# Pinning the adaLN products of a hybrid decoder layer's mixer to slots in program order

## The chip, the cores and the metric

The kernel runs on one core of one Trainium2 chip. The metric is the device time of one execution in microseconds (us), as the median of several runs. Besides, one execution was recorded by the hardware profiler; its span runs from the first to the last instruction of the program.

## The reference, cut to what matters

One decoder layer for 256 tokens of width 1024, in float32. Three blocks follow each other, and each is fed by a normalised and modulated copy of the stream and gated back into it:

```python
mod = (c @ w_ada + b_ada).reshape(B, 9, D_MODEL)
sh1, sc1, g1, sh2, sc2, g2, sh3, sc3, g3 = [mod[:, None, i] for i in range(9)]
h = modulate(rmsnorm(x, ffn1_norm), sh1, sc1)
x = x + 0.5 * (1 + g1) * swiglu(h, ...)
h = modulate(rmsnorm(x, mix_norm), sh2, sc2)
x = x + (1 + g2) * hybrid_mixer(h, ...)
h = modulate(rmsnorm(x, ffn2_norm), sh3, sc3)
x = x + 0.5 * (1 + g3) * swiglu(h, ...)
return rmsnorm(x, final_norm)
```

The mixer projects h to q, k, v of an attention with 8 heads (one causal block of 256 tokens here), to x_m of an mLSTM with 4 heads (a causal convolution of 4 taps, a decay matrix, scores times decay, a normalisation) and to a gate z. The attention's output and the mLSTM's, the latter times silu(z), are concatenated and multiplied by w_out.

## The kernel before, in words

**Layout.** Channels lie on the 128 partitions and the 256 tokens on the free axis. The stream x is 8 tiles of 128x256, and the modulated copy h is kept as a high part `hh` and a low part `hl` of 8 tiles each, with two more columns for the shift.

**Products in three passes.** Every weight product (`mm3`) is three matmuls on TensorE: high weight by high input, low weight by high input, high weight by low input. Weights come in chunks of 128x2048 (`raw`, 4 buffers). `split_piece` (line 201) turns half a chunk into a high part `whi` on ScalarE (one copy) and a low part `wlo` on VectorE (one subtraction), with 5 buffers of 128x1024 for each. `weights()` (line 221) issues the loads up to three chunks ahead and the splits up to one chunk ahead of the chunk that it hands out.

**The adaLN products.** `mod` has 72 columns of 128. Each is one job: `ada(col)` (line 247) loads 128x1024 of w_ada (512 KB) into one of three `ada` buffers and forms the dot product with c in one VectorE instruction, whose full-size output `junk` is thrown away and whose sum goes to one column of `mod`. After 8 columns a few small instructions make the scale `gs`, the shift `sh` or the gate `gt`. The jobs stand in a list (line 571), and `side(...)` (line 564) takes one off it for each of its arguments; so the calls of `side` in the program say where a job is issued. In the mixer these calls stand at lines 933 to 1026; the first two calls belong to the product of x_m (line 579). The jobs left at that time are the gate of block 2, the scale `gs[2]` and the shift `sh[2]` of block 3.

**What sets the order.** A scheduler with its own timing model orders the instructions of each engine while the program is built (`schedule_with_timeline_sim`, line 42); what it decided is fixed then, and on the chip each engine takes its list in order. An instruction that was handed to `keep_in_program_order` is not moved against the others that were handed to it. All loads are (so SyncE's list is the program's order); of the compute engines' instructions those that were issued while the wrapper `Ordered` (line 45) was on for the engine. In the mixer it is off but for a stretch around `a_out` and `m_factors`. Each buffer has a few slots, so an instruction may also wait for a slot: a load of `ada` waits for the product that read the same slot three jobs before.

**The mixer's steps** (line 601 on). `tiles` runs one chunk of w_in as two products of 8 x 3 matmuls into a PSUM bank `psb`; `shifted` finishes such a product with a copy of the shift column (`col`, ScalarE), a product with the reciprocal root `rr` (`ht`, VectorE) and a copy with bias (ScalarE), and frees the bank. The rest is small: `gates` and `decays` make `rows` and the decay tiles `wE` from a chain on 4 partitions; `decays` spreads `rows` over two PSUM banks (TensorE, `psm<-rows,ohr`), subtracts into `wE` (VectorE, 8 instructions) and applies exp (ScalarE). `m_scores` multiplies keys by queries into a bank of the same pair (`psm<-qk,xc`) and the result into `wE`. `scores`, `turn`, `weigh` are the attention. The last chunk of w_in gives z; after it come `m_factors` (chain `dd`, `vv`, `rs` on 4 partitions, then `rows` again), `z_silu` in two halves, and `hilo` of the attention's output tiles `oa` into `hh`/`hl` 1 to 3, which hold h until the last product of z has read it. Then w_out runs in 8 steps of 24 matmuls: step 0 reads `mix0h`/`mix0l`, steps 1 to 3 read the attention's tiles in `hh`/`hl`, steps 4 to 7 the mLSTM's (`m_out`). Then `pre_shift(2)` writes the shift `sh[2]` into the extra columns of `hh`/`hl`, and `residual` adds the product to x and makes h of block 3.

Of the kernel before, what the change touches and what calls it, by code (L numbers as in the profile page):

```python
# [14 lines left out]
ALU = mybir.AluOpType  # L15
# [46 lines left out]
def layer(ctx: ExitStack, tc: tile.TileContext, i, out: bass.AP):  # L62
    nc = tc.nc
    act, dve, pool, pe = (Ordered(tc, e) for e in (nc.scalar, nc.vector, nc.gpsimd, nc.tensor))
# [14 lines left out]
    def nm(s):  # L79
        cnt[0] += 1  # L80
        return f"{s}_{cnt[0]}"
# [3 lines left out]
    def bank(tag):  # L85
        return psp.tile([P, 512], F32, tag=tag, name=nm("ps" + tag), bufs=BANKS[tag])
# [7 lines left out]
    def const(shape, dt, name):  # L94
        return cst.tile(shape, dt, tag=name, name=name)

    def dma(out, in_):
        return tc.keep_in_program_order(sp.dma_start(out, in_))  # L98
# [26 lines left out]
    c_bc = const([P, D], F32, "c_bc")  # L125
# [95 lines left out]
    def weights(ahead=3):  # L221

        n = used[0]
        used[0] += 1
        load_to(n + ahead)
        split_to(n + 1)
        return parts[n]
# [6 lines left out]
    def mm3(ps, w, b0, xh, xl, start, stop):  # L234
        hi, lo = part(w, b0, P)
        pe.matmul(ps, hi, xh, start=start, stop=False, skip_group_check=True)
        pe.matmul(ps, lo, xh, start=False, stop=False, skip_group_check=True)
        pe.matmul(ps, hi, xl, start=False, stop=stop, skip_group_check=True)


    mod = const([P, 72], F32, "mod")
# [2 lines left out]
    gt = [const([P, ND], F32, f"gt{k}") for k in range(3)]  # L244
    NCOL = [C_N1, C_N2, C_N3]

    def ada(col, on_pool=False):

        t = wp.tile([P, D], F32, tag="ada", name=nm("ada"), bufs=3)
        dma(t, i["ada"][col])  # L250
        junk = wp.tile([P, D], BF16, tag="junk", name=nm("junk"), bufs=1)
        dve.scalar_tensor_tensor(junk, t, 1.0, c_bc, ALU.mult, ALU.mult,
                                 accum_out=mod[:, col:col + 1])

    def ada_gate_fin(k):
        s0 = 24 * k + 16
# [40 lines left out]
    def rstd_of(parts, ones=None, tag="m", pre=True, mid=None):  # L297

        ps = bank(tag)[:, 0:T]
        for n, s in enumerate(parts):  # L300
            pe.matmul(ps, ones_m if ones is None else ones, s, start=(n == 0), stop=(n == len(parts) - 1))
        r = t256("rr", bufs=2)
        l = t256("rl", bufs=1)
        if pre:
            tables("natural_log_exp_and_others")
        act.activation(l, ps, AF.Ln, bias=eps_t)
        act.activation(r, l, AF.Exp, scale=-0.5)
        if mid:
            mid()
        newton(r, ps, [P, T], "x")  # L310
        return r
# [90 lines left out]
    def ffn(k, nxt):  # L402
        nfa = 3
        with tc.tile_pool(name=f"g{k}", bufs=1) as gp:
            g2 = gp.tile([P, NF, 2, T], F32R, name=f"g2{k}")
            gh, gl = g2[:, :, 0], g2[:, :, 1]
            if k == 0:
                half = gp.tile([P, 8, 2 * T], F32, name="half")

                def adas(d):  # L410
                    ada(d, d > 0)
                    ada(8 + d)
# [151 lines left out]
    def side(*on):  # L564

        for o in on:
            if jobs:
                jobs.pop(0)(o)
# [5 lines left out]


    px = [bank("a") for _ in range(4)]
    for c in range(2):
        w = weights()
        side(1, 0)
        for d4 in range(4):  # L580
            d = c * 4 + d4
            for h in range(NH):
                mm3(px[h][:, 0:W], w, d4 * 512 + h * P, hh[:, d], hl[:, d], start=(d == 0), stop=(d == 7))
            if d == 0:
                r = rstd_of([acc, nxt_sq[0]], pre=False)
    with tc.tile_pool(name="mix", bufs=1) as mp:
        mixer(tc, nc, i, mp, locals())


    with tc.tile_pool(name="fin", bufs=1) as fp:  # L590
# [10 lines left out]
def mixer(tc, nc, i, mp, L):  # L601
    act, dve, pool, pe, sp = L["act"], L["dve"], L["pool"], L["pe"], L["sp"]
# [6 lines left out]
    side, jobs = L["side"], L["jobs"]  # L609
# [4 lines left out]
    def tiles(*done):  # L614

        w = weights()
        for g in range(2):
            pb = bank("b")
            for d in range(8):
                mm3(pb[:, 0:W], w, (g * 8 + d) * P, hh[:, d], hl[:, d], start=(d == 0), stop=(d == 7))  # L620
            done[g](pb)
            yield

    def shifted(dst):

        def done(pb):
            col = tmp.tile([P, 1], F32, tag="col", name=nm("col"), bufs=3)
            act.activation(col, pb[:, T:T + 1], AF.Copy)
            t = t256("ht", bufs=3)
            dve.tensor_tensor(t, r, pb[:, 0:T], ALU.mult)  # L630
            act.activation(dst, t, AF.Identity, bias=col)
        return done
# [16 lines left out]
    def fold():  # L649

        pg = bank("a")
        for h in range(NH):
            pe.matmul(pg[:, h * 40:(h + 1) * 40], wT[:, h], wif[:, h * 3], start=(h == 0), stop=False,
                      skip_group_check=True)
            pe.matmul(pg[:, h * 40:(h + 1) * 40], wT[:, 4 + h], wif[:, h * 3 + 1], start=False, stop=True,
                      skip_group_check=True)
            pe.matmul(pg[:, 160 + h * 40:160 + (h + 1) * 40], wT[:, 8 + h], wif[:, h * 3 + 2], start=False,
                      stop=True, skip_group_check=True)
        act.activation(wfold[:, 0:320], pg[:, 0:320], AF.Copy)
        pqk = bank("a")  # L660
        for h in range(NH):
            pe.matmul(pqk[:, h * P:(h + 1) * P], wT[:, h], wT[:, 4 + h], start=(h == 0), stop=(h == NH - 1),
                      skip_group_check=True)
        act.activation(wfold[:, 320:832], pqk, AF.Copy, scale=float(P) ** -0.5)

        vmean = mt([P, NH], "vmean")
        dve.tensor_reduce(vmean, wv0, AX.X, ALU.add)
        dve.tensor_scalar(vmean, vmean, 1.0 / P, None, ALU.mult)
        for h in range(NH):
            dve.tensor_scalar(wv[:, h], wv0[:, h], vmean[:, h:h + 1], None, ALU.subtract)  # L670
# [134 lines left out]
    def m_factors():  # L805


        prow, em = st["prow"], st["em"]
        act.on = dve.on = True
        dd = mt([NH, T], "dd", tag="R2")  # L810
        act.activation(dd, prow[0:4, 0:T], AF.Square, scale=EPS ** 0.5)
        dve.tensor_tensor(dd, dd, em, ALU.max)
        vv = mt([NH, T], "vv", tag="R3")
        dve.scalar_tensor_tensor(vv, prow[0:4, T:2 * T], 1.0 / P, dd, ALU.mult, ALU.add)
        rs = mt([NH, T], "rs", tag="R1")
        act.activation(rs, vv, AF.Ln)
        act.activation(rs, rs, AF.Exp, scale=-0.5)
        newton(rs, vv, [NH, T], "r", 0.0)
        spread(rs)
# [4 lines left out]
    def mix(k):  # L824
        return mix0 if k == 0 else (hh[:, k, 0:T], hl[:, k, 0:T])
# [3 lines left out]
    def z_silu(h2):  # L829
        z2 = zs[:, 2 * h2:2 * h2 + 2]  # L830
        tc.keep_in_program_order(act.activation(z2, z2, AF.Silu))
# [23 lines left out]
    def queries(j):  # L855
        qa, ka = st["qk", j] = mt([P, T], "qa", bufs=2), mt([P, T], "ka", bufs=2)
        return tiles(shifted(qa), shifted(ka))
# [31 lines left out]
    def values(c):  # L889
        v = [t256("gm"), t256("gm")]  # L890
        yield from tiles(shifted(v[0]), shifted(v[1]))
        pt = bank("a")
        for s in range(2):
            for g in range(2):
                pe.transpose(pt[:, (s * 2 + g) * P:(s * 2 + g + 1) * P], v[g][:, s * P:(s + 1) * P], ident)
        act.activation(va[:, :, c * T:(c + 1) * T], pt.rearrange("p (s c) -> p s c", s=2), AF.Copy)
        yield
# [39 lines left out]
    conv(1)  # L937
    next(g)
    fold()
    side(1, 0)  # L940
    g = queries(1)
    conv(2)
    next(g)
    conv(3)
    next(g)
    g0 = values(0)
    side(0, 1)
    next(g0)
    gates()
    next(g0)  # L950
    scores(0)
    m_queries()
    g = queries(2)
    side(0, 1)
    next(g)
    next(g0)
    m_values()
# [2 lines left out]
    scores(1)  # L960
    turn(0)
    g = queries(3)
    side(0, 1)
    next(g)
    weigh(0)
    m_scores(0)
# [3 lines left out]
    scores(2)  # L970
    m_scores(2)
    g0 = values(1)
    side(0, 1)
    next(g0)
    weigh(1)
    scores(3)
# [3 lines left out]
    m_scores(3)  # L980
    m_sums(1)
    g = tiles(shifted(zs[:, 0]), shifted(zs[:, 1]))
    side(1, 0, 0)
    next(g)
    next(g0)
    turn(3)
# [10 lines left out]
    m_vars(1)  # L997
    m_vars(2)
    g = tiles(shifted(zs[:, 2]), shifted(zs[:, 3]))
    side(1)  # L1000
    next(g)
    m_vars(3)
    m_factors()
    z_silu(0)
    next(g)
    for j in range(1, 4):
        hilo(*mix(j), oa[:, j, 0:T])
    z_silu(1)
    for h in range(NH):
        m_out_pre(h)  # L1010
# [1 line left out]
    po = [bank(t) for t in ("m", "m", "a", "a")]  # L1012
    for c in range(4):
        w = weights()
        side(0)
        pe.on = c < 2
        for k2 in range(2):
            k = c * 2 + k2
            for d in range(8):
                mm3(po[d // 2][:, (d % 2) * T:(d % 2 + 1) * T], w, (k2 * 8 + d) * P, *mix(k),  # L1020
                    start=(c == 0 and k2 == 0 and d % 2 == 0), stop=(c == 3 and k2 == 1))
                if (k, d) == (2, 7):
                    m_spread()
                    for h in range(NH):
                        m_out(h)
    side(*[0] * len(jobs))
    L["pre_shift"](2)
    for d in range(8):
        nxt_sq[0] = residual(d, po[d // 2][:, (d % 2) * T:(d % 2 + 1) * T], L["gt"][1], 2)

# [85 lines left out]
```

## Time and profile before

| | |
|---|---|
| median of 3 runs | 543.53 us (543.39 to 544.7) |
| the profiled execution's own time | 542.25 us |
| its span | 540.5 us |
| TensorE busy (matmul) | 516.9 us, 96% of the span |
| VectorE busy | 424.1 us, 78% |
| ScalarE busy | 282.6 us, 52% |
| moved by DMA | 125.73 MB, mean 233 GB/s |

The page's columns: PE is TensorE's matmul, PEld its weight load, DVE VectorE, ACT ScalarE, POOL GpSimd, SP SyncE. Times are from the span's start. Nearly every compute instruction has line 55 (the wrapper), so instructions are told apart by their tiles. In the timeline a row's second number is the time of the instructions that it merges, and "x8" counts the profiler's records: an fp32 matmul leaves two or more. The end of a matmul is modelled, so its start to the next one's start is the safer reading. The first block lasts to about 205 us, the mixer to about 340, the second feed-forward block to the end.

### The profile page before, as it was taken

To read this page: it belongs to the slowest core of one execution; us is meant where nothing else is said; L and a number is where in the kernel's file an instruction comes from. 1 tells how busy PE (TensorE), PEld (TensorE's weight loads), DVE (VectorE), ACT (ScalarE), POOL (GpSimd) and SP (SyncE) were. 2 spreads that over 40 slices of the span, in tenths; PEclk is the share of its full clock that TensorE was granted. 3 is DMA by queue.
4 is the path that set the end of the run, shared out by engine and by line. 5 is a ranking of instruction groups with operands and counts; after the bars stand their busy time and mean duration, and the time that the engine had idled before them with its cause. 6 is when DMAs were issued, how large, how long until landed. Compare 5 with 4: busy or idle time off the path is not lost.

```text
span 540.5 us, 9607 instructions
## 1 busy us (share of the span) xinstructions
PE 516.9 (96%) x3826; PEld 484.0 (90%) x3826; DVE 424.1 (78%) x717; ACT 282.6 (52%) x484; POOL 46.2 (9%) x60
## 2 busy tenths in 40 slices
PE   8999999999999999999969969999999999999992
PEld 7899999999988889978856869999999999988892
DVE  7899978988799988997894666979987777655433
ACT  4364456665554454648655544965554554544410
POOL 5000000000010210200010000400000000012320
PEclk9999999999999999999999979999999999999997
DMA  8999986587788985776771114387855455455002
GB/s 314 352 368 396 372 333 235 212 303 276 278 345 320 346 340 180 266 297 235 308 275 42 50 69 136 101 349 292 312 202 206 178 169 211 167 181 209 1 1 78
DMA packets 24095, 125.73 MB, mean 233 GB/s; under 512 B 2673, under 2 KB 3185, under 8 KB 14578
## 3 DMA queue, kind: packets, MB, share of 16 engines
q1 hardware_dynamic: 23762, 124.72, 61.6%
q8 instruction: 30, 0.49, 0.4%
q10 hardware_dynamic: 288, 0.39, 0.2%
q14 instruction: 15, 0.12, 0.1%
HBM read 124.05 MB, written 1.05 MB: 231 GB/s over the span
## 4 chain that ended last, share of the span: by engine, by line
PE 89%; DVE 4%; DMA 2%; ACT 2%; issue 1%; SPq 0%; DVEq 0%; ACTq 0%
PE psa L55 45%; PE psb L55 25%; PE psm L55 20%; DMA ada<-in_ada 2%; DVE junk L55 1%; ACT whi L55 1%; DVE wE L55 1%; DVE wlo L55 0%; DVE ht L55 0%; DVE u_out L55 0%; SPq L98 0%; ACT hh L55 0%; ACT L55 0%; ACT zs L55 0%; DVE nw L55 0%
## 5 line engine op out<-in xcount | busy, mean ns | idle before, releaser
L55 ACT ACTIVATE whi<-raw 128x1024 fp32r<-128x1024 f32 (+1 forms) x160 | 166.8, 1047 | 133.1 <-PE psa L55 83.4
L55 DVE TENSOR_TENSOR wlo<-raw,whi 128x1024 fp32r<-128x1024 f32 (+1 forms) x160 | 193.8, 1215 | 50.3 <-ACT whi L55 48.7
L55 PE MATMUL psa<-hh,wlo 128*128 128x256 f32 (+1 forms) x452 | 127.2, 282 | 0.0
L55 PE MATMUL psa<-hh,whi 128*128 128x256 f32 (+1 forms) x452 | 127.0, 283 | 0.0
L55 PE MATMUL psa<-hl,whi 128*128 128x256 f32 (+1 forms) x452 | 126.1, 281 | 0.0
L55 DVE SCALAR_TENSOR_TENSOR junk<-ada,c_bc 128x1024 bf16<-128x1024 f32 x72 | 89.4, 1242 | 8.3 <-DMA ada<-in_ada 7.7
L55 PEld LDWEIGHTS psa<-hh,wlo 128*128 128x128 f32 x452 | 85.9, 190 | 0.1
L55 PEld LDWEIGHTS psa<-hh,whi 128*128 128x128 f32 x452 | 85.7, 190 | 0.0
L55 PEld LDWEIGHTS psa<-hl,whi 128*128 128x128 f32 x452 | 85.5, 190 | 0.0
L55 PE MATMUL psb<-hh,whi 128*128 128x258 f32 (+1 forms) x284 | 81.6, 288 | 0.6 <-ACT whi L55 0.6
L55 PE MATMUL psb<-hh,wlo 128*128 128x258 f32 (+1 forms) x284 | 80.2, 283 | 0.6 <-DVE wlo L55 0.6
L55 PE MATMUL psb<-hl,whi 128*128 128x258 f32 (+1 forms) x284 | 79.8, 283 | 0.0
L55 PE MATMUL psa<-g,whi 128*128 128x512 f32 (+1 forms) x198 | 59.8, 369 | 0.0
L55 PEld LDWEIGHTS psb<-hh,whi 128*128 128x128 f32 x284 | 53.7, 189 | 2.7 <-issue 1.0
L55 PEld LDWEIGHTS psb<-hh,wlo 128*128 128x128 f32 x284 | 53.8, 189 | 0.9 <-DVE wlo L55 0.8
L55 PEld LDWEIGHTS psb<-hl,whi 128*128 128x128 f32 x284 | 53.5, 189 | 0.2 <-issue 0.2
L55 PE MATMUL psm<-hh,whi 128*128 128x256 f32 (+1 forms) x168 | 48.1, 287 | 4.8 <-ACT hh L55 4.8
L55 PE MATMUL psm<-hh,wlo 128*128 128x256 f32 (+1 forms) x168 | 47.8, 285 | 0.0
L55 PE MATMUL psm<-hl,whi 128*128 128x256 f32 (+1 forms) x168 | 47.5, 285 | 0.0
L55 PE MATMUL psa<-g,wlo 128*128 128x256 f32 x176 | 45.9, 281 | 0.0
L55 PEld LDWEIGHTS psa<-g,whi 128*128 128x128 f32 x198 | 35.2, 188 | 6.2
L55 PEld LDWEIGHTS psm<-hh,whi 128*128 128x128 f32 x168 | 32.5, 194 | 5.1 <-ACT hh L55 5.0
(238 smaller groups left out, 759.5 us busy)
## 6 DMA issues: line engine op xcount, KB each, us to landing
ada<-in_ada SPq DMA_DIRECT2D x72, 512.0 KB, 5.8
raw<-in_dn SPq DMA_DIRECT2D x22, 1024.0 KB, 4.8
raw<-in_guB SPq DMA_DIRECT2D x19, 1024.0 KB, 4.8
raw<-in_gu SPq DMA_DIRECT2D x18, 1024.0 KB, 6.4
raw<-in_gu SPq DMA_DIRECT2D x8, 512.0 KB, 7.3
raw<-in_wqk SPq DMA_DIRECT2D x4, 1024.0 KB, 5.4
raw<-in_wout SPq DMA_DIRECT2D x4, 1024.0 KB, 6.8
raw<-in_guA SPq DMA_DIRECT2D x4, 768.0 KB, 4.0
```

What stands on the lines that cost most here:

```text
L55: r = f(*a, **k)
```

## The change

The change has five edits. (1) While `pinned[0]` is true, that is from the product of x_m to the mixer's end, each adaLN product is handed to `keep_in_program_order`. (2) The calls of `side` are dealt out anew: fewer jobs at the start of the mixer and among the attention's products, five ahead of the first chunk of z, four ahead of the second, three in w_out's loop. (3) `z_silu(0)` moves behind the `hilo` of the attention's tiles. (4) w_out's loop takes no job in its first two turns and two, then three (as far as there are any) in its last. (5) `pre_shift(2)` runs with the wrapper on, for ScalarE and VectorE.

```diff
+    pinned = [False]
...
-        dve.scalar_tensor_tensor(junk, t, 1.0, c_bc, ALU.mult, ALU.mult,
-                                 accum_out=mod[:, col:col + 1])
+        p = dve.scalar_tensor_tensor(junk, t, 1.0, c_bc, ALU.mult, ALU.mult, accum_out=mod[:, col:col + 1])
+        if pinned[0]:
+            tc.keep_in_program_order(p)
...
     px = [bank("a") for _ in range(4)]
+    pinned[0] = True
     for c in range(2):
         w = weights()
-        side(1, 0)
+        side(*[0] * (2 - c))
...
         mixer(tc, nc, i, mp, locals())
+
+    pinned[0] = False
...
     fold()
-    side(1, 0)
+    side(0)
...
     g0 = values(0)
-    side(0, 1)
+    side(0)
...
     g = tiles(shifted(zs[:, 0]), shifted(zs[:, 1]))
-    side(1, 0, 0)
+    side(0, 0, 0, 0, 0)
...
     g = tiles(shifted(zs[:, 2]), shifted(zs[:, 3]))
-    side(1)
+    side(0, 0, 0, 0)
     next(g)
     m_vars(3)
     m_factors()
-    z_silu(0)
     next(g)
     for j in range(1, 4):
         hilo(*mix(j), oa[:, j, 0:T])
+    z_silu(0)
     z_silu(1)
...
     for c in range(4):
         w = weights()
-        side(0)
+        side(*[0] * c if c > 1 else ())
...
     side(*[0] * len(jobs))
+    act.on = dve.on = True
     L["pre_shift"](2)
+    act.on = dve.on = False
```

The scheduler then orders everything else anew. Three places follow; the numbers behind the names count buffers and differ between the two programs for the same tile.

VectorE, from the last attention maxima ahead of the decay tiles to the first scores times decay. Before:

```order
L55 COPY nac_2549<-psm_3010 128x8
L55 SCALAR_TENSOR_TENSOR junk_3406,mod<-ada_3404,c_bc 128x1024
L55 TENSOR_TENSOR em_2872<-nM_2868,F_2864 4x256
L55 TENSOR_TENSOR rows_2545<-nM_2868,rows_2545 4x256
L55 TENSOR_REDUCE mx_3315<-psa_3305 128x1 x2
L55 TENSOR_SCALAR mx_3224<-mx_3224 128x4
L55 TENSOR_TENSOR ht_3445<-rr_2420,psb_3418 128x256
L55 TENSOR_REDUCE mx_3315<-psa_3306 128x1 x2
L55 SCALAR_TENSOR_TENSOR junk_3551,mod<-ada_3549,c_bc 128x1024
L55 TENSOR_TENSOR wlo_3560<-raw_3256,whi_3559 128x1024
L55 TENSOR_SCALAR em_2872<-em_2872 4x256
L55 SCALAR_TENSOR_TENSOR wE_394_2550<-psm_3014,nac_2549,maskt 128x256
```

With the change:

```order
L55 TENSOR_TENSOR rows_2541<-nM_2856,rows_2541 4x256
L55 TENSOR_SCALAR pr_3062<-pr_3062,ri_3064 128x256
L55 SCALAR_TENSOR_TENSOR junk_3090,mod<-ada_3088,c_bc 128x1024
L55 TENSOR_SCALAR em_2860<-em_2860 4x256
L55 TENSOR_TENSOR ht_3129<-rr_2420,psb_3102 128x256
L55 COPY nac_2545<-psm_2994 128x8
L55 TENSOR_TENSOR wlo_3236<-raw_2936,whi_3235 128x1024
L55 TENSOR_TENSOR ht_3176<-rr_2420,psb_3149 128x256
L55 SCALAR_TENSOR_TENSOR wE_392_2546<-psm_2998,nac_2545,maskt 128x256
```

The first decay tile (wE) moved forward against the products of w_in: it stood behind the `ht` of the first product of z (psb_3418), and now stands behind that of the second half of q and k 3 (psb_3149), three products earlier. Ahead of it VectorE's list holds 11 adaLN products (`junk`) fewer than before; behind it, up to the end of w_out, 13 where there were 2. TensorE's list has the spreading of `rows` directly ahead of the first scores before (`psm<-rows,ohr`, then `psm<-qk,xc`), and with the change 14 matmuls of a product of w_in and 11 small ones of the attention between the two.

ScalarE, behind the chain of `m_factors`. Before:

```order
L55 ACTIVATE whi_3726<-raw_3553 128x1024
L55 ACTIVATE rows_2545<-rs_3599 4x256
L55 ACT_TABLE_LOAD
L55 ACTIVATE zs_2557<-zs_2557 128x512
L55 ACTIVATE col_3634<-psb_3609 128x1
L55 ACTIVATE zs_2557<-ht_3636,col_3634 128x256
L55 ACTIVATE hh<-oa_2559 128x256 x3
```

With the change:

```order
L55 ACTIVATE whi_3718<-raw_3549 128x1024
L55 ACTIVATE rows_2541<-rs_3595 4x256
L55 ACTIVATE col_3629<-psb_3604 128x1
L55 ACTIVATE zs_2553<-ht_3631,col_3629 128x256
L55 ACTIVATE hh<-oa_2555 128x256 x3
L55 ACT_TABLE_LOAD
L55 ACTIVATE zs_2553<-zs_2553 128x512 x2
```

The table load and the first silu stood between `rows` and the last `col`; they now stand behind the three `hh` tiles. On VectorE the same stretch, from the `ht` of the second product of z on, holds with the change:

```order
L55 TENSOR_TENSOR ht_3520<-rr_2420,psb_3493 128x256
L55 SCALAR_TENSOR_TENSOR junk_3535,mod<-ada_3533,c_bc 128x1024
L55 TENSOR_TENSOR ht_3586<-rr_2420,psb_3559 128x256
L55 SCALAR_TENSOR_TENSOR junk_3539,mod<-ada_3537,c_bc 128x1024
L55 TENSOR_TENSOR wlo_3661<-raw_3392,whi_3660 128x1024
L55 TENSOR_TENSOR dd_3590<-dd_3590,em_2860 4x256
L55 SCALAR_TENSOR_TENSOR junk_3543,mod<-ada_3541,c_bc 128x1024
L55 SCALAR_TENSOR_TENSOR vv_3593<-psa_3306,dd_3590 4x256
L55 SCALAR_TENSOR_TENSOR junk_3547,mod<-ada_3545,c_bc 128x1024
```

The four `junk` rows are new there; before, that list ran without them, and behind `vv` it held the two small instructions of `pre_shift`, which are now behind the last `ht` of w_out. On SyncE's list the loads of these four products (ada_3533 to ada_3545) now stand ahead of the load of w_out's third chunk (raw_3549), and five others ahead of its second.

## Rows read from the trace of the kernel before

**Rows 1.** Waits of TensorE from 205 to 360 us: total, times, longest.
```profile
PE psm L55 <- DVE wE L55: 4.9, 2, 4.2
PE psm L55 <- ACT hh L55: 4.8, 1, 4.8
```

**Rows 2.** Stretches: length, PE, PEld, DVE, ACT, POOL busy, PEclk, DMA share, GB/s.
```profile
232.00:260.00 28.00, 28.00 (x201) 23.33 (x198) 24.47 (x52) 20.12 (x47) 0.18 (x1) 1.00 0.74 278
276.00:287.00 11.00, 6.06 (x26) 4.32 (x25) 10.94 (x31) 7.19 (x24) 0.00 (x0) 0.84 0.55 210
287.00:311.00 24.00, 24.00 (x170) 19.35 (x169) 11.03 (x27) 13.16 (x32) 0.72 (x1) 1.00 0.09 32
304.20:314.20 10.00, 7.59 (x60) 6.81 (x58) 6.28 (x12) 6.61 (x13) 0.00 (x0) 1.00 0.22 79
316.50:322.50 6.00, 5.95 (x27) 5.95 (x28) 4.26 (x11) 1.52 (x4) 0.00 (x0) 0.50 0.17 65
322.50:330.00 7.50, 7.50 (x62) 7.24 (x62) 5.47 (x12) 3.58 (x6) 0.00 (x0) 0.99 0.07 11
```

**Rows 3.** Timeline of TensorE around the first wait: start, us, instruction, idle before.
```profile
277.12 0.73 PE L55 MATMUL psm<-rows,ohr 36*128 36x256 f32 x4
282.05 2.95 PE L55 MATMUL psm<-qk,xc 128*128 128x256 f32 x8 [4.20 <-DVE wE L55]
285.74 0.92 PE L55 MATMUL psm<-qk,xc 128*128 128x256 f32 x4 [0.74 <-DVE wE L55]
```

**Rows 4.** Timeline of VectorE in the same place.
```profile
278.15 1.22 DVE L55 SCALAR_TENSOR_TENSOR junk<-ada,c_bc 128x1024 bf16<-128x1024 f32 x1
279.29 1.23 DVE L55 TENSOR_TENSOR wlo<-raw,whi 128x1024 fp32r<-128x1024 f32 x1
280.62 2.67 DVE L55 SCALAR_TENSOR_TENSOR wE<-psm,nac,maskt 128x256 f32<-128x256 f32 x8
```

**Rows 5.** Timeline of TensorE around the second wait.
```profile
311.51 0.28 PE L55 MATMUL psa<-mix0l,whi 128*128 128x256 f32 x1
316.55 0.58 PE L55 MATMUL psm<-hh,whi 128*128 128x256 f32 x1 [4.75 <-ACT hh L55]
```

**Rows 6.** Timeline of ScalarE in the second wait.
```profile
311.83 1.06 ACT L55 ACTIVATE whi<-raw 128x1024 fp32r<-128x1024 f32 x1 [0.98 <-PE psa L55]
313.21 1.28 ACT L55 ACT_TABLE_LOAD   x1
314.50 0.63 ACT L55 ACTIVATE zs<-zs 128x512 f32<-128x512 f32 x1
315.04 0.15 ACT L55 ACTIVATE col<-psb 128x1 f32<-128x1 f32 x1
```

**Rows 7.** Timeline of VectorE ahead of and in the second wait, parts.
```profile
305.56 0.42 DVE L55 TENSOR_TENSOR ht<-rr,psb 128x256 f32<-128x256 f32 x1 [1.37 <-ACT col L55]
...
312.92 1.23 DVE L55 TENSOR_TENSOR wlo<-raw,whi 128x1024 fp32r<-128x1024 f32 x1 [0.35 <-ACT whi L55]
314.18 0.41 DVE L55 TENSOR_TENSOR rows<-rs,rows 4x256 fp32r<-4x256 f32 x1
315.23 0.42 DVE L55 TENSOR_TENSOR ht<-rr,psb 128x256 f32<-128x256 f32 x1 [0.64 <-ACT col L55]
```

**Rows 8.** DMA issues from 205 to 365 us: count, KB each, median us to landing.
```profile
ada<-in_ada SPq DMA_DIRECT2D x22, 512.0 KB, 3.7
raw<-in_wout SPq DMA_DIRECT2D x4, 1024.0 KB, 6.8
```

**Rows 9.** Timeline of VectorE and TensorE in w_out's later steps and behind them.
```profile
328.85 0.76 DVE L55 TENSOR_TENSOR hl<-ht,hh 128x256 fp32r<-128x256 f32 x2
...
340.31 0.48 DVE L55 SCALAR_TENSOR_TENSOR hl<-x,gs,hh 128x256 fp32r<-128x256 f32 x1
...
329.63 0.28 PE L55 MATMUL psm<-hl,whi 128*128 128x256 f32 x1
...
341.02 0.40 PE L55 MATMUL psb<-hl,whi 128*128 128x258 f32 x2
```

More of the change, by code (lines that the diff above doesn't have):

```diff
@@ L953, in mixer @@
     g = queries(2)
-    side(0, 1)
+    side(0)
     next(g)
@@ L962, in mixer @@
     g = queries(3)
-    side(0, 1)
+    side(0)
     next(g)
@@ L972, in mixer @@
     g0 = values(1)
-    side(0, 1)
+    side(0)
     next(g0)
```

## The prediction

> **What bounds the kernel now.** I read the waits of TensorE first, because the page has it busy for 96% of the span. In the mixer they name only two places [rows 1]: 4.9 us of waiting for the decay tiles `wE`, in two pieces, and one wait of 4.8 us for the tiles `hh` that feed w_out. Everywhere else there TensorE has work, so the change can gain at these two waits, and it can lose by making new ones.
>
> The busy shares by stretch come second [rows 2]. From 232 to 260 us VectorE is busy for 24.47 of 28 us and TensorE without a gap; from 276 to 287 VectorE for 10.94 of 11 us and TensorE for only 6.06. From 287 to 311 it turns round: VectorE has 11.03 of 24 us to do, and DMA is at 9%. So VectorE is late when the decay tiles are due and has 13 us to spare right behind that.
>
> The timelines give the causes. **First wait:** TensorE spreads `rows` at 277.12, and its next items are scores that need a bank which the eight subtractions into `wE` must have read [rows 3]. VectorE begins these at 280.62, since its list has an adaLN product at 278.15 and a `wlo` at 279.29 ahead of them [rows 4]. TensorE stands for 4.20 us, then for 0.74. The scores behind the first piece run slowly: 8 records in 2.95 us, where 4 take 0.92 a little later [rows 3]; the granted clock is 0.84 on average over the stretch [rows 2], which with two levels means 1.2 GHz for part of it. At the later pace 8 records are 1.84 us, so the slow clock costs another 1.1.
>
> **Second wait:** step 0 of w_out ends at 311.51, and step 1 begins at 316.55 [rows 5]. In between ScalarE does, in its order, `whi` (311.83), `rows`, the table load (313.21), the silu (314.50), and only at 315.04 the `col` of the last product of z [rows 6]; VectorE does `ht` at 315.23 [rows 7], and then the `hh` tiles may be written. Behind it the granted clock is 0.50 for 6 us, 27 matmuls in 5.95 us or 0.220 each, against 0.121 in the next stretch (62 in 7.50) [rows 2]; 27 x 0.099 = 2.7 us.
>
> **The change part by part.** One adaLN product holds VectorE for 1.14 us (278.15 to 279.29) [rows 4].
>
> *A, the first wait.* The order has 11 products fewer ahead of `wE`: 11 x 1.14 = 12.5 us of VectorE's work. The wait is 4.9 us, and TensorE gets 14 matmuls (0.12 each, 1.7 us) and small items as cover between spreading `rows` and the scores. I take the whole: 4.20 + 0.74 + 1.1 = **6.0 us gained**. Lower bound: VectorE still has much of its list crowded against `wE`, and half goes, 3.0. Upper bound: 6.0; there is no more to remove.
>
> *B, the new order of the attention.* The scheduler has set all items from 215 to 305 us anew, and some copies and maxima now stand closer to those who need them. The trace does not show that order. Bounds: nothing lost, as with VectorE 87% busy from 232 to 260 and no gap on TensorE [rows 2]; or a loss like the 0.74 piece [rows 3] four times, 3.0. I take one such piece, **0.8 lost**, because most banks have their matmuls in hand long before.
>
> The five products ahead of the first chunk of z fall into 287 to 311: 5 x 1.14 = 5.7 us into 13 us of idle VectorE, cost 0 for TensorE unless B's upper bound comes. Their loads, 5 x 512 KB at 3.7 us each [rows 8], come where DMA was at 9% [rows 2]; that cover is large.
>
> *C, the second wait.* The table load and the silu leave ScalarE's chain: 313.21 to 315.04, 1.8 us [rows 6]. But VectorE is next in line: its `rows` at 314.18 stands ahead of `ht` at 315.23 [rows 7], so even with ScalarE out of the way `ht` begins at about 314.52, which is 0.7 earlier and no more. On the other side four products come into this very stretch. From 304.20 to 314.20 VectorE is idle for 10.00 - 6.28 = 3.72 us [rows 2]; 4 x 1.14 = 4.56 overshoots that by 0.8, less the two small instructions of `pre_shift` that leave, and some of the idle time lies where a product can't use it, as the 1.37 ahead of the `ht` at 305.56 that a load may miss [rows 7]. So `ht` would come between 0.7 earlier and 1.5 later than before; I take **0**, and the slow clock behind it stays.
>
> Taken by the trace, TensorE's clock falls behind a wait of 4.2 or 4.75 us and not behind the 0.74 [rows 2, 3, 5]; between those I know nothing. The Trainium skill's page "TensorE: Matmul & The Clock Gate", section "Part 1: The HAM clock gate (the "warmup" mystery)", says that the array's clock is set by how busy the engine has been recently and falls to half when it idles; by that, a somewhat shorter second wait could still be a slow one, as I assume, or could just escape, which is a rival below.
>
> *SyncE's queue.* The third chunk of w_out is now loaded behind four adaLN loads that share three buffers; the fourth must wait for the first of the four products, which by VectorE's idle time ends about 305.3. With 6.8 us from issue to landing [rows 8] the chunk is there at 312.1, about when `whi` would start (311.83) [rows 6]. Cost 0.3, inside C's range.
>
> *D, w_out's later steps.* One product now stands ahead of the `hl` of step 4 on VectorE. That `hl` starts at 328.85, and TensorE reads one of its kind at 329.63, without a gap [rows 9]. A product is 1.14, and of the 0.78 between them about half is the instruction itself. So between 0 and 1.1 is lost; I take **0.5**. The other two products in the loop lie in idle time of VectorE (5.47 busy of 7.50 [rows 2]).
>
> *E, the end of the mixer.* The last step's banks end in another order, and VectorE adds a third residual ahead of the first `hl`. Before, `hl` at 340.31 led to the first matmul on it at 341.02 [rows 9]. I put a residual at the 0.48 of the `hl` beside it, which has the same form and size [rows 9]. Between 0 and three of them, 1.5; I take one, **0.5**. `pre_shift` under the wrapper is two instructions of 8 columns: 0, covered by VectorE's idle time in the loop; without cover 0.3, at the 0.15 of the smallest ScalarE instruction for each [rows 6].
>
> **Sum.** 6.0 - 0.8 - 0 - 0.5 - 0.5 = 4.2 us gained. The profiled execution took 542.25 (span 540.5, 1.75 around it), which becomes 538.05. The median of the runs is 543.53, 1.28 above the profiled one; I keep that: 543.53 - 4.2 = **539.3 us**.
>
> **The rivals.** *R1, the clock holds at the second wait.* If it shrinks by the full 0.7 or more, and the clock does not fall, 2.7 + 0.7 = 3.4 more is gained: 535.9. For it: the table load is the largest single item there. Against: four products crowd the same stretch. Chance 0.13.
>
> *R2, half the first wait stays.* The attention's work is set closer together, VectorE runs nearly full from 287 to 311 too (11.03 + 8 x 1.14 = 20.2 of 24 us), and B costs its 3.0 instead of 0.8, or A gives only half; 4.2 - 2.6 = 1.6 gained: 541.9 with both at the middle, up to 543.5 with both bad. For it: TensorE's items between 287 and 311 have had an idle VectorE to lean on and now have not. Against: 232 to 260, 87% busy without a gap [rows 2]. Chance 0.18.
>
> *R3, slower.* The third chunk of w_out stands behind four loads on three buffers. If the first of the four products is late, the fourth load is, and so is the chunk; and ScalarE, which takes its list in order, holds `rows`, `col` and the `hh` tiles behind `whi`. From the start of `whi` to step 1 of w_out it is 316.55 - 311.83 - 1.8 = 2.9 us. To eat the 4.2 gained elsewhere and 1.6 more, step 1 must begin at 322.4, so the chunk must land at 319.5, and the first of the four products end at 319.5 - 6.8 = 312.7 instead of 305.3. That would be 545.3 or more. For it: the queue is in order and only three buffers deep. Against: VectorE's 3.7 us of idle time and nothing but an `ht` ahead of that product. Chance 0.08.
>
> *R4, more headroom than the waits show.* From 232 to 260 the weight load is busy for 23.33 of 28 us and from 287 to 311 for 19.35 of 24, while in w_out it is 7.24 of 7.50 [rows 2]; if the difference were lost time that a better order gives back, 97% of the two stretches less what they have would be 7.7 us more: 531.6. Against: TensorE shows no wait there, and short products with few columns load less weight for each matmul. Chance 0.03. The Trainium skill's "Perfetto Trace Analysis", section "Identifying the Most-Contended Engine", judges TensorE by its weight loads rather than by its matmul row, which is this reading.
>
> That the change does not do what it says is excluded: the built order has the products where the diff puts them.
>
> **How the numbers follow.** My forecast has 0.58, its own range 537.5 to 541.5 (B, C, D and E at better or worse ends, not all together). A measurement here can tell 0.3%, or 1.6 us, from no change: faster is below 541.9, slower above 545.1. Faster: forecast 0.56, R1 0.13, R4 0.03 and a third of R2, 0.06: 0.78. Same: the rest of R2, 0.12, and 0.02 of the forecast: 0.14. Slower: R3, 0.08. The range takes in R1's 535.9 and most of R2: 535.0 to 543.3, leaving out R3, R4 and the tail of R2.
>
> **What would show it.** A: no wait of TensorE on `wE` over 1 us, and a granted clock of 1.00 through that stretch. B: at most a handful of waits under 1 us between 215 and 305. C: a wait for `hh` of 4 to 5.5 us and again a clock of 0.50 behind it; if VectorE's `ht` is what ends it and not ScalarE, the term is right in its mechanism. D and E: new waits on `hl` of about 0.5 us. The prediction is wrong if `wE` still holds TensorE for 2 us or more, or if the wait for `hh` is under 3.5 us, or if w_out waits for a load.

## The result and the profile after

The change makes the kernel 1.4% faster: 536.07 us (median of 4 runs, 535.7 to 536.19) against 543.61 before (543.39 to 544.7), a ratio of 0.9856 with a 95% interval of 0.9839 to 0.9873. The forecast was 539.3 with a range of 535.0 to 543.3: the right side and inside the range, but the gain is 7.5 us and not 4.2.

| | before | after |
|---|---|---|
| median | 543.61 us | 536.07 us |
| the profiled execution's own time | 542.25 | 536.01 |
| its span | 540.5 | 534.2 |
| granted clock over the span | 0.985 | 0.988 |
| TensorE busy (matmul) | 516.9 | 513.6 |

The waits of TensorE from 205 to 360 us after the change (engine and tile, released by, total, times, longest; compare [rows 1]):

```profile
PE psm L55 <- ACT hh L55: 4.7, 1, 4.7
PE psa L55 <- ACT va L55: 1.4, 1, 1.4
PE psm L55 <- DVE hl L55: 0.7, 1, 0.7
PE psb L55 <- DVE hl L55: 0.3, 1, 0.3
PE psa L55 <- DVE x L55: 0.2, 1, 0.2
```

The waits on `wE` are gone, the wait for `hh` is the same to 0.1 us, and four small ones are new. Where the time came from is read best from what TensorE begins when. The timeline of TensorE before, at the fold ahead of the attention and at the start of w_out:

```profile
220.32 2.77 PE L55 MATMUL psa<-wif,raw 128*128 128x40 f32 x24
...
308.76 0.28 PE L55 MATMUL psm<-mix0h,whi 128*128 128x256 f32 x1
...
328.69 0.28 PE L55 MATMUL psm<-hh,whi 128*128 128x256 f32 x1
...
340.05 0.28 PE L55 MATMUL psb<-hh,whi 128*128 128x258 f32 x1
```

The last two rows are the start of w_out's step 4 and the first matmul behind w_out, which reads a new `hh`. The same with the change, with the spreading of `rows`, the first scores that need its banks, step 1 of w_out, the wait at step 4 and the first matmul on the new `hl`:

```profile
220.54 2.77 PE L55 MATMUL psa<-wif,raw 128*128 128x40 f32 x24
...
261.33 0.50 PE L55 MATMUL psm<-rows,ohr 36*128 36x256 f32 x2
...
265.50 0.81 PE L55 MATMUL psm<-qk,xc 128*128 128x256 f32 x4
...
301.59 0.28 PE L55 MATMUL psm<-mix0h,whi 128*128 128x256 f32 x1
...
309.35 0.58 PE L55 MATMUL psm<-hh,whi 128*128 128x256 f32 x1 [4.73 <-ACT hh L55]
...
320.53 0.28 PE L55 MATMUL psm<-hh,whi 128*128 128x256 f32 x1
...
322.31 0.39 PE L55 MATMUL psm<-hl,whi 128*128 128x256 f32 x1 [0.68 <-DVE hl L55]
...
332.82 0.28 PE L55 MATMUL psb<-hh,whi 128*128 128x258 f32 x1
...
334.86 0.39 PE L55 MATMUL psb<-hl,whi 128*128 128x258 f32 x1 [0.25 <-DVE hl L55]
```

From the fold to w_out's first step it was 88.44 us and is 81.05: 7.4 gained. From there to step 1 it was 7.79 [rows 5] and is 7.76. From step 1 to the first matmul on the new `hl` it was 24.47 [rows 5, 9] and is 25.51: 1.0 lost. With the 0.2 by which the fold itself starts later, that leaves 6.2 us in the two profiled executions; the rest of the 7.5 is between the median and the profiled execution, below.

The 1.0 lost in w_out is a balance of three. From step 1 to step 4 it was 12.14 [rows 5] and is 11.18: 1.0 gained, where the clock is low for a shorter time (below). From step 4 to the first matmul behind w_out it was 11.36 and is 12.29: 0.9 lost, at the wait of 0.68 for `hl`. From there to the first matmul on the new `hl` it was 0.97 [rows 9] and is 2.04: 1.1 lost, at the waits on `x` and `hl`. The idle times in the list of waits are smaller than these losses, since idle time counts from the modelled end of a matmul and these are taken from start to start.

VectorE with the change, where the decay tiles are made (compare [rows 4]):

```profile
259.18 1.20 DVE L55 TENSOR_TENSOR wlo<-raw,whi 128x1024 fp32r<-128x1024 f32 x1
261.42 0.42 DVE L55 TENSOR_TENSOR ht<-rr,psb 128x256 f32<-128x256 f32 x1 [1.03 <-ACT col L55]
261.86 1.39 DVE L55 SCALAR_TENSOR_TENSOR wE<-psm,nac,maskt 128x256 f32<-128x256 f32 x4
```

VectorE has 1 us to spare ahead of them, and begins them half a microsecond after TensorE has begun to spread `rows` (261.33); the first scores that need the bank come at 265.50. The second wait, on ScalarE and VectorE:

```profile
304.10 2.00 ACT L55 ACTIVATE whi<-raw 128x1024 fp32r<-128x1024 f32 x2 [0.30 <-DMA raw<-in_wout]
306.01 0.40 ACT L55 ACTIVATE rows<-rs 4x256 fp32r<-4x256 f32 x1
306.31 0.14 ACT L55 ACTIVATE col<-psb 128x1 f32<-128x1 f32 x1
308.48 0.51 ACT L55 ACTIVATE zs<-ht,col 128x256 f32<-128x256 f32 x1 [2.02 <-DVE ht L55]
```

```profile
305.20 2.35 DVE L55 TENSOR_TENSOR wlo<-raw,whi 128x1024 fp32r<-128x1024 f32 x2
307.58 0.42 DVE L55 TENSOR_TENSOR rows<-rs,rows 4x256 fp32r<-4x256 f32 x1
308.02 0.42 DVE L55 TENSOR_TENSOR ht<-rr,psb 128x256 f32<-128x256 f32 x1
```

ScalarE now idles for 2.02 us in front of the last `zs` and waits for VectorE, which is held by two `wlo` of w_out's third chunk; that chunk was issued at 298.57 behind the last of the four adaLN loads, and `whi` waited for it until 304.10. So the silu's place on ScalarE should hardly matter any longer, and nothing is won. Behind the wait the clock falls as before, for a shorter time:

```profile
309.30:314.00 4.70, 4.65 (x24) 4.65 (x25) 3.21 (x9) 3.04 (x5) 0.00 (x0) 0.57 1.02 419
314.00:318.00 4.00, 4.00 (x33) 3.73 (x32) 2.81 (x6) 1.93 (x2) 0.00 (x0) 1.00 0.32 126
```

(The columns are those of [rows 2].) With two levels, 0.57 over 4.70 us is 4.0 us at 0.50. Before it was 0.50 for the whole of 6 us [rows 2].

### The profile page after: what moved, and what is told of

Same layout as the page of the kernel before. It is cut to its first block, busy times and chain, and to the rows that moved or that the text cites. A ratio compares the mean times of both kernels' runs of the same rounds, so it can differ in the third digit from the quotient of the medians.

```text
span 534.2 us, 9598 instructions
## 1 busy us (share of the span) xinstructions
PE 513.6 (96%) x3826; PEld 481.8 (90%) x3826; DVE 425.7 (80%) x717; ACT 281.9 (53%) x484; POOL 46.9 (9%) x60
## 4 chain that ended last, share of the span: by engine, by line
PE 88%; DVE 4%; DMA 4%; ACT 2%; issue 1%; SPq 0%; DVEq 0%; ACTq 0%
PE psa L55 44%; PE psb L55 24%; PE psm L55 20%; DMA raw<-in_gu 2%; DMA ada<-in_ada 1%; DMA raw<-in_wout 1%; ACT whi L55 1%; DVE wlo L55 1%; DVE junk L55 1%; DVE x L55 1%; DVE ht L55 0%; SPq L98 0%; DVE u_out L55 0%; DVE nw L55 0%; DVE oa L55 0%
```

## The experiments

Each was compared with the kernel before on the same chip, whose median was 543.5 to 544.3 there. The numbers in the table are the medians and the ratios with their 95% intervals.

| run | us | ratio |
|---|---|---|
| e1_slots_only | 541.85 | 0.9967 [0.9948, 0.9985] |
| e2_pin_only | 535.90 | 0.9870 [0.9831, 0.9910] |
| e3_silu_back | 536.64 | 0.9882 [0.9843, 0.9920] |
| e4_scores_apart | 537.44 | 0.9895 [0.9864, 0.9926] |
| e9_loop_back | 535.52 | 0.9854 [0.9820, 0.9887] |
| e6_hilo_first | 536.50 | 0.9871 [0.9840, 0.9902] |
| e10_lean | 537.21 | 0.9880 [0.9848, 0.9913] |
| e11_lean_scores | 537.42 | 0.9892 [0.9850, 0.9935] |
| e12_chain | 529.95 | 0.9753 [0.9720, 0.9785] |
| e14_chain_scores | 531.47 | 0.9782 [0.9753, 0.9811] |

### Slots or pinning?

e1_slots_only is the change without its pinning:

```diff
-    pinned[0] = True
+    pinned[0] = False
```

> The change without the pinning: the calls of side stand as in the change, but the adaLN products may be moved by the scheduler. In the order that it built, 61 products stand ahead of the first wE (62 before, 51 with the change), and the spreading of rows is again directly ahead of the scores. Theory P (the number of products ahead of wE sets the first wait, and only pinning lowers it): TensorE waits 3 to 5 us for wE, time 541 to 544. Rival S (the new slots do it by themselves, through the loads that come later): no wait on wE over 1 us, time about 536 to 537.

e2_pin_only is the kernel before with the pinning alone:

```diff
...
-        dve.scalar_tensor_tensor(junk, t, 1.0, c_bc, ALU.mult, ALU.mult,
-                                 accum_out=mod[:, col:col + 1])
+        p = dve.scalar_tensor_tensor(junk, t, 1.0, c_bc, ALU.mult, ALU.mult, accum_out=mod[:, col:col + 1])
+        if pinned[0]:
+            tc.keep_in_program_order(p)
...
+    pinned[0] = True
     for c in range(2):
         w = weights()
         side(1, 0)
```

> Before with the pinning alone, the calls of side as before. 56 products stand ahead of the first wE, 6 fewer than before and 5 more than with the change. Theory P: 6 x 1.14 = 6.8 us less work ahead of wE is more than the wait of 4.9, so the wait on wE falls below 1 us and most of the gain is there: 536.5 to 539. Rival S: nothing gained without the new slots, a wait of 3 us or more on wE, 542 to 544.

The waits of TensorE in e1, and then in e2:

```profile
PE psm L55 <- ACT hh L55: 5.5, 1, 5.5
PE psm L55 <- DVE wE L55: 4.4, 1, 4.4
```

```profile
PE psm L55 <- ACT hh L55: 5.3, 1, 5.3
PE psa L55 <- POOL acc L55: 0.3, 1, 0.3
```

Theory P holds in both. Without pinning the new slots move one product (61 ahead of `wE` instead of 62), the wait is 4.4, and some 2 us are gained in the median, though only 0.4 between the spans of the profiled executions. With pinning and the old slots, 56 are ahead, the wait is gone, and the whole gain is there; the time of 535.90 is even a little under P's 536.5. The reason, as I read it, is what `keep_in_program_order` does, which the section on the kernel before put too strongly: it places an instruction behind the one that was issued just before it on its engine, and so forbids only that it is moved forward. No run tests that reading by itself. An adaLN product depends on its load alone, so the scheduler moved it forward, ahead of work that TensorE needs. The slots were there before; they were not kept.

One thing more changes with the pinning, in e2 as in the change: TensorE now has other matmuls between the spreading of `rows` and the first scores (4.2 us from start to start with the change, 6.2 in e2), where before it had none. Before, the first scores began 1.43 us behind the first subtraction [rows 3, 4]; with a subtraction that starts 0.53 behind the spreading, scores right behind the spreading would by this estimate still have waited some 1.3 us. So VectorE's earlier start is most of what ended the wait of 4.2, and TensorE's new order may be the rest; no run holds one of them fixed.

Edits 2 to 5 together, which are most of the diff, are worth nothing that can be told on top of the pinning (536.07 against 535.90): by the start of TensorE's steps it gains 1.5 us in the attention (82.55 in e2, 81.05 with the change) and 0.6 at the second wait, and gives 2.3 back in w_out (23.20 in e2, 25.51 with the change).

### The silu's place

e3_silu_back undoes edit 3:

```diff
     m_factors()
+    z_silu(0)
     next(g)
     for j in range(1, 4):
         hilo(*mix(j), oa[:, j, 0:T])
-    z_silu(0)
     z_silu(1)
```

> The change with only the silu of z's first half put back ahead of the last product of z's finish. In the trace of the change the wait for hh runs over the load of w_out's third chunk (landed 304.0), two whi, two wlo until 307.5, rows and ht at 308.0; ScalarE was free at 306.45 for 2.0 us. Theory V (VectorE and the load end this wait, ScalarE has 1.6 us of slack): table load and silu cost 0.2 to 0.6 us, time 536.2 to 536.8. Rival A (ScalarE's chain ends it, the move gained its 1.8): 537.6 to 538.2.

The wait for `hh` is 5.17 instead of 4.73, the time 536.64: theory V. The load and VectorE end this wait; moving 1.8 us of ScalarE's work out of it gained 0.4 by the wait, a difference that the two times can't tell by themselves.

### What the clean waits don't show: two halves of the scores

The waits on `wE`, their slow clock and the new wait for `va` don't add up to 7.4. So I took every group of TensorE's matmuls from the fold to w_out and summed the time from its start to the next start. The scores of the attention (`psa<-ka,qa`, 32 records) took 6.15 us before and 4.42 with the change, in stretches without a wait and at a granted clock of 1.00. Two rows show why. With the change:

```profile
231.37 0.93 PE L55 MATMUL psa<-ka,qa 64*128 64x128 f32 x8
232.24 0.40 PE L55 MATMUL psa<-maskq,ident_b 128*128 128x128 bf16 x4
```

Eight records take 0.87. Four alone also take 0.85: in e4_scores_apart, which holds the two halves of each pair of heads apart,

```diff
+        pe_on, pe.on = pe.on, True
         for e in range(2):
             rw = slice(e * 64, e * 64 + 64)
...
-        for e in range(2):
             pe.matmul(ps[e][:, 0:P], ident_b, maskq, start=False, stop=True, skip_group_check=True)
             pe.matmul(ps[e][:, T:384], ident_b, maskq, start=False, stop=True, skip_group_check=True)
+        pe.on = pe_on
```

> The change with the two halves of each head pair's scores (keys on partitions 0 to 63 and on 64 to 127) held apart on TensorE by the mask's matmuls, pinned. Theory O (the two halves use different rows of the array and overlap when they stand side by side: 8 records in 0.86 us, 4 alone also in 0.86): 4 pairs at 1.72 to 1.8 us instead of 4.42 in all, so 2.5 to 2.8 us more for them and 538 to 539. Rival N (the pitch is set by something else, as the bank or the queue): the records take 4.4 us as in the change, and the time stays at 535.7 to 536.6.

the timeline reads

```profile
239.22 0.92 PE L55 MATMUL psa<-ka,qa 64*128 64x128 f32 x4
240.07 0.28 PE L55 MATMUL psa<-maskq,ident_b 128*128 128x128 bf16 x2
240.28 0.92 PE L55 MATMUL psa<-ka,qa 64*128 64x128 f32 x4
241.13 0.29 PE L55 MATMUL psa<-maskq,ident_b 128*128 128x128 bf16 x2
```

The first head of a pair has its keys on partitions 0 to 63, the second on 64 to 127. Side by side the two overlap; with a matmul of 128 rows between them they don't. All 32 records take 6.90 us here instead of 4.42, as theory O had it. The kernel takes 1.4 us longer in the median and 1.2 in the span, less than O's 538 to 539: the wait for `va` fell from 1.36 to 0.60, so not all of it arrives. The two halves also write different PSUM banks, and no run parts the partitions from the banks as the reason. The change got its 1.73 us only because the scheduler happened to put the halves side by side in two of the four pairs and in part of a third; before, it did so in part of two pairs. And the kernel does not need it for its gain: in e2 the scores take 6.15 us as before.

### The end of w_out

e9_loop_back undoes edits 4 and 5:

```diff
-        side(*[0] * c if c > 1 else ())
+        side(0)
...
-    act.on = dve.on = True
     L["pre_shift"](2)
-    act.on = dve.on = False
```

> The change with its two edits in w_out's loop undone: one job in each turn as before, the third pre-shift without the wrapper. Theory D/E (the products ahead of step 4's hl and in the last turn make the new waits of 0.68 on hl, 0.16 on x and 0.25 on hl): these waits go, against one product more ahead of the hl tiles of step 1 (0 to 0.5), time 534.8 to 535.8. Rival L (they hide behind the wait for hh or come from the scheduler's new order): no change, 535.8 to 536.5.

The time is 535.52, inside what D/E expected, but only half of it for the reason given: the waits on `x` and the last `hl` are gone, and from the first matmul behind w_out to the first on the new `hl` it is 0.97 again instead of 2.04; the wait at step 4 stays at 0.73. VectorE shows why, directly ahead of the tiles of step 4, with the change and then in e9:

```profile
320.36 1.22 DVE L55 SCALAR_TENSOR_TENSOR junk<-ada,c_bc 128x1024 bf16<-128x1024 f32 x1
```

```profile
320.35 1.22 DVE L55 SCALAR_TENSOR_TENSOR junk<-ada,c_bc 128x1024 bf16<-128x1024 f32 x1
```

An adaLN product stands in this place in both, so e9 did not take away what D is about. The difference of 0.5 in time is no more than these intervals can tell.

### Can the second wait be taken away?

The wait for `hh` is most of what TensorE still waits in the mixer (4.7 of 7.2 us), and nothing in it is bound to happen: the last product of z is done when step 0 begins. e6_hilo_first moves `next(g)` and `hilo` ahead of `m_factors()` in the change, with the wrapper on:

```diff
     m_vars(3)
-    m_factors()
+    act.on = dve.on = True
     next(g)
     for j in range(1, 4):
         hilo(*mix(j), oa[:, j, 0:T])
+    m_factors()
     z_silu(0)
```

> The change with one step moved: the last product of z is finished and hh and hl of the attention's tiles are written ahead of the chain of m_factors; the splits of w_out's third and fourth chunk stay where the scheduler wants them. Theory K alone: no wait for hh, clock 1.00, 6 to 7 us gained, 529 to 530. Rival M (rows and the silu now stand behind four whi and four wlo and come some 5 us later, so w_out waits at m_spread or at step 4): the wait goes from hh to rows or hl with 3 to 6 us, time 533 to 537.

e10_lean does it on e2_pin_only, with `rows` (`spread`) and the silu behind `hilo`, the splits of w_out's third chunk behind them, and three adaLN products in w_out's last turn alone (`newton` and `spread` are taken out of `m_factors`):

```diff
     g = tiles(shifted(zs[:, 2]), shifted(zs[:, 3]))
-    side(1)
     next(g)
+    w0 = weights()
     m_vars(3)
     m_factors()
-    z_silu(0)
     next(g)
+    rs, vv = st["rs"]
+    newton(rs, vv, [NH, T], "r", 0.0)
     for j in range(1, 4):
         hilo(*mix(j), oa[:, j, 0:T])
+    spread(rs)
+    z_silu(0)
     z_silu(1)
...
     for c in range(4):
-        w = weights()
-        side(0)
+        act.on = dve.on = c == 1
+        w = weights() if c else w0
+        act.on = dve.on = False
+        side(*[0] * 3 if c == 3 else ())
```

> Before with the pinning, and the second wait taken apart: the last product of z is finished and the attention's tiles are split into hh and hl ahead of rows and the silu, the splits of w_out's third chunk stand behind them (pinned), and three adaLN products stand in w_out's last turn. Theory K (the wait for hh is only order on ScalarE and VectorE, and the slow clock follows from it): the wait of 5.3 falls below 1 us, the granted clock stays at 1.00 in w_out; 5 + 1.7 gained on 535.9, time 528.5 to 531. Rival M (the wait moves on: rows and the tiles of step 4 come later and hold w_out there): a wait of 3 us or more behind step 2 or 3, and the clock falls there, 533 to 536.

The first wait for `hh` vanishes in both, and neither is faster than what it came from. The wait moves on. In e6:

```profile
PE psb L55 <- DVE rows L55: 2.9, 1, 2.9
PE psm L55 <- ACT hh L55: 2.6, 1, 2.6
```

In e10 it is 2.30 at step 4, and at the end of w_out there are small ones. VectorE in e10 shows the cause at step 4, three `wlo` ahead of the first `ht`:

```profile
310.88 3.49 DVE L55 TENSOR_TENSOR wlo<-raw,whi 128x1024 fp32r<-128x1024 f32 x3
314.29 1.08 DVE L55 TENSOR_TENSOR ht<-cn,psb 128x256 f32<-128x256 f32 x3
```

and the clock comes down later (the columns of [rows 2]):

```profile
325.00:333.00 8.00, 6.58 (x51) 5.97 (x51) 7.81 (x18) 5.67 (x16) 2.37 (x4) 1.00 0.56 216
333.00:338.00 5.00, 4.77 (x26) 4.56 (x27) 5.00 (x8) 3.79 (x8) 3.78 (x4) 0.66 0.06 23
```

So rival M held in kind: the wait moves on. In e6 its sizes are as M had them; in e10 the wait is under M's 3 us, the clock falls only at the end of w_out, and the time is above M's 533 to 536. e11_lean_scores adds the program's order for the scores to e10:

> The same, and the attention's scores issued in the program's order, so that more of the two halves stand side by side on TensorE. Theory O (halves overlap): 1 to 1.7 us off the scores' 6.14, time 0.8 to 1.7 below the run with the label e10_lean. Rival N (the new order around them costs what it gains): within 0.5 of it.

It is 0.2 us slower than e10. The scores do come closer together (5.13 us instead of 6.14), but a wait of 1.43 for `pr` is new, rival N. e12_chain then orders what e10 left to chance. For each head the tiles are made in the order in which w_out reads them, and each `wlo` stands in its turn. The three adaLN products of w_out's last turn move ahead of z's first chunk, and `pre_shift` runs with the wrapper on; so what is gained belongs to these edits together:

```diff
-    side(1, 0, 0)
+    side(*[0] * 6)
...
-                if (k, d) == (2, 7):
+                if (k, d) == (1, 7):
                     m_spread()
-                    for h in range(NH):
-                        m_out(h)
+                    act.on = dve.on = True
+                    split_piece(True)
+                    split_piece(True)
+                    m_hi(0)
+                    late.pop(0)()
+                    m_hi(1)
+                    m_lo(0)
+                    m_out_pre(2)
+                    late.pop(0)()
+                    m_lo(1)
...
```

(`m_hi` and `m_lo` are the two halves of `m_out`; `split_piece(True)` does the `whi` and puts the `wlo` into `late`.)

> As e10_lean, and the tiles of w_out's steps 4 to 7 made one after the other in the order in which they are needed: rows are spread after step 1, each high part and low part and each wlo of the third chunk pinned in its turn, the fourth chunk's splits behind them, the three adaLN products moved from w_out's last turn to those ahead of z's first chunk, the pre-shift pinned. Theory M (in e10_lean the wait moved on to step 4 because three wlo stood ahead of its tiles on VectorE, and the clock fell there): with the waits of 2.3 and 0.5 at step 4 and of 1.6 at the end of w_out gone or under 0.5 each, the granted clock stays at 1.00 from 230 us on, 528.5 to 531. Rival G (the time goes somewhere else whatever the order, for a chain of loads or of VectorE's work): a new wait of 2 us or more, 534 to 537.

All the waits of TensorE from 205 to 360 us that are left in e12, and w_out in its stretches:

```profile
PE psa L55 <- DVE x L55: 0.3, 1, 0.3
PE psa L55 <- POOL acc L55: 0.3, 1, 0.3
```

```profile
300.00:310.00 10.00, 10.00 (x80) 9.62 (x80) 7.19 (x18) 7.61 (x16) 0.00 (x0) 1.00 0.52 191
310.00:320.00 10.00, 10.00 (x87) 10.00 (x87) 9.19 (x19) 4.25 (x8) 0.00 (x0) 1.00 0.23 79
320.00:330.00 10.00, 9.71 (x78) 9.20 (x77) 9.80 (x19) 7.17 (x16) 1.59 (x2) 1.00 0.71 249
```

The granted clock is 1.00 all through, and the time 529.95: 6.1 us under the change, 14 under the kernel before. e14_chain_scores adds the program's order for the scores, with the wait for `pr` of 1.43 again, and is 1.5 slower, at the very end of what was expected:

> As e12_chain, with the scores issued in the program's order. In e11_lean_scores that brought the scores closer together and a wait of 1.43 for pr. Expected the same here: within 1.5 of e12_chain, and not faster by more than 0.5.

## Why the prediction was right, and where it was off

- **What bounds the kernel** was right: two waits, the first from a VectorE with too much ahead of `wE`. e1 and e2 show that pinning and not the slots takes the first wait away, and that the number of adaLN products ahead of `wE` goes with it. Wrong was that time can be gained at the two waits only.
- **A**, 6.0 predicted. From the spreading of `rows` to the next start TensorE lost 4.11 less, and over the scores of the mLSTM (`psm<-qk,xc`) 2.56 less: 6.7 in all.
- **B**, 0.8 lost predicted, as one piece like the 0.74: it is one piece of 1.36, for `va`, above the 1 us that was named as the sign.
- **C**, 0 predicted with VectorE as the engine that ends the wait: 4.75 became 4.73, and the chain is the one described. The third chunk's load, forecast for 0.3 us behind the time at which `whi` wants it, held `whi` for 0.30 (the 304.10 row above). By its letter that is the sign "w_out waits for a load", but what ended TensorE's wait was the chain through VectorE's `ht`. This was the step with the most in it, and it held, but for the clock: "the slow clock behind it stays" came true for 4.0 us and not for 6, which gave back 1.0.
- **D** and **E**, 0.5 each predicted, have the waits that were forecast (0.68 on the `hl` of step 4, 0.16 and 0.25 at the end), but were mis-sized: from start to start they cost 0.9 and 1.1. For E, e9 takes the cause away and the loss goes; for D the product ahead of the tiles stands in the row at 320.36, and no run removes it.
- **R1**, that the clock might hold at the second wait, did not happen, nor did R2 and R3; in e12, where the wait itself is gone, the clock does hold. R2's upper end doesn't follow from its parts: with both bad, 4.2 - 2.2 - 3.0 is -1.0, or 544.5 and not 543.5.

The sum is 3.3 us short, 2.0 between the two profiled executions (6.2 gained, 4.2 forecast) and 1.3 from there to the median. The 2.0 is a balance: 1.7 from the scores, 1.0 from the shorter slow stretch and 0.7 in A came on top, 0.6 in B and 1.0 in D and E went off, and the rest is small. That the miss of D and E and the gift of the clock cancel is luck.

The largest of these is **a term that the sum did not have**: the 1.7 us of the scores. I had read "TensorE without a gap" as time that can't be won. R4 argued the other way and got a chance of 0.03, since I took the low weight-load share for short products; part of that share was halves that could have run side by side, though 1.7 us of them and not 7.7. B should have asked what the new order does to TensorE's own pitch, and not only to its waits.

The other part is **the step from the profile to the median**: "1.28 above the profiled one; I keep that". After the change it is 0.06. The 1.28 probably belonged to the slow clock behind the waits: executions of the kernel before lie between 540.8 us at a granted clock of 0.986 and 545.0 at 0.979, and the profiled one had 0.985. The change's four lie within 0.5 us. e1, which keeps the first wait, shows a longer slow stretch behind it than the profile of before does (there the scores were back at their later pace at 285.74 [rows 3]):

```profile
281.10:286.00 4.90, 4.80 (x14) 3.69 (x15) 4.68 (x19) 3.19 (x11) 0.00 (x0) 0.50 0.35 138
```

So the one profile may have caught a short one, and the first wait may have cost the median more than it cost the profile. This is argued from the clocks, and no run separates it: e9, which has only the second wait, also spreads, from 534.6 us at 0.992 to 536.4 at 0.987.

## What to carry to other kernels

Where a scheduler orders the instructions, check that work without haste stays where it was written: here products that depend on a load alone were moved forward until they stood ahead of what the bound engine waits for, and one pin each did what a new table of slots did not. A wait that ends a long chain is taken away only when the next tiles of that chain are ordered as well: e6 and e10 removed it and gained nothing, e12 put the following ten microseconds in order and gained 6. And an engine that is busy without a gap may still be slow: sum start-to-start times by kind of instruction, not only idle times.

## What the hardware showed that I had not expected

- Two fp32 matmuls of 64 rows on different halves of the partitions overlap when they stand next to each other in TensorE's list: 8 records in 0.87 us, and 4 alone in 0.85. (The two write different banks as well.)
- The clock behind a wait does not depend on the length of that wait alone. Behind the waits for `hh` of 4.75 us (before), 4.73 (the change) and 5.30 (e2) it was low for some 6 us, 4.0 and 3.4 (0.57 over 3.90): for the shortest time behind the longest wait. Behind the same wait of 2.30 at step 4 it was low at once in e11, and in e10 it stayed at 1.00 for over 15 us and then fell behind waits of 0.2 to 0.7. The stretches behind the wait in e2, e11 and e10 (the columns of [rows 2]):

```profile
311.10:315.00 3.90, 3.86 (x20) 3.86 (x21) 3.88 (x12) 1.32 (x5) 0.00 (x0) 0.57 0.14 58
```

```profile
319.20:322.20 3.00, 3.00 (x14) 3.00 (x15) 2.97 (x7) 0.58 (x2) 0.00 (x0) 0.50 1.01 399
```

```profile
317.30:325.00 7.70, 7.19 (x58) 6.99 (x59) 6.52 (x13) 2.58 (x5) 0.00 (x0) 1.00 0.87 309
```
